# Tiles padded to 64 bytes and three norm factors moved into the exponentials' scales, in a decoder layer on one core

## The chip, the cores and the metric

One Trainium2 chip, of which one NeuronCore runs the kernel. The metric is the device time of one execution in microseconds (us); "time" of a kernel is the median of its runs. The engines are TensorE (PE in the profile, its weight loads PEld), VectorE (DVE), ScalarE (ACT), GpSimd (POOL) and SyncE (SP), which here issues nearly all DMAs.

## What is computed

The reference is one decoder layer for 256 tokens of width 1024, in float32. Cut to what matters here:

```python
hn = rmsnorm(h, mix_norm_g); proj = hn @ w_in            # q, k, v, conv, gates
h = h + concat([conformer_conv(...), nsa_mixer(q, ...)]) @ w_out
h = h + memory_attention(rmsnorm(h, g), rmsnorm(mem, g2), w_q, w_k, w_v, w_o)
h = h + peer(rmsnorm(h, peer_norm_g), w_q, sub_keys, u_emb, v_emb)
return rmsnorm(h, final_norm_g)
# in each attention: softmax((q @ k.T) * scale); in peer: top 16 of 16 x 16 candidate
# pairs for each token and head, softmax over those scores, experts u and v (16384 x 1024)
```

`rmsnorm` multiplies each token by one factor r = 1/sqrt(mean(x*x) + eps) (and each column by a gain). A query that is projected from a normed row is therefore r times the query projected from the unnormed row, and so are its scores.

## The kernel before, in words

Tokens stand in the free dimension (256 columns), features in the partitions. A product in nearly float32 precision is made of three `float32r` matmuls: every operand is split in a high part (a rounding copy on ACT) and a low part (a subtraction on DVE), and `mm3` (L151 to L154) issues high x high, low x high and high x low into one PSUM tile. `wchunk` (L147) loads 512 KB of weights into a tile `raw` and splits it in two halves (`wsplit`, L134 to L145: `hi` L141 on ACT, `lo` L142 on DVE, or on POOL where it is told so); `hi` and `lo` have six buffers each, three chunks deep. In `mm3` the weights are the stationary operand and the 256 token columns move; in the last stage (L1071) the activations `ah`, `al` are stationary and the weights move, 512 columns a matmul.

TensorE's order is the program's (a manual schedule for that engine alone); the other engines' instructions are put in order by the scheduler of the tile framework. The stages are:

- the input projection (`proj1`, plain float32 matmuls of two passes, L163) with the conformer convolution on DVE, then the sparse attention (`scores` L548, `transposes`, `weighted`), into which the key and value projections of the memory attention are filled (`filler`, L432: tiles `pmk`, `pmv`);
- `w_out` (tiles `pwo`), the queries of the memory attention (`mq_chunk`, `mq_out`, L718 to L727, tiles `pmq`), its scores `pms` (L735 to L737) and weighted sums `pmo` (through `mm3`), `w_mem_o` (tiles `pmw`);
- the 16 chunks of the expert queries (L846, tiles `ppq`), each copied out of PSUM by `pq_out` (L829) and matched with the keys by `key_scores` (L834);
- the choice of the 16 best experts on DVE (L893 to L954) while TensorE goes through the first of the 128 chunks of `u` (`u_chunk`, L987, tiles `pu`): for chunks 0 to 33 POOL makes the low parts, from chunk 34 (`JG`) on DVE does. From chunk 41 on `gates4` (L1003) comes in between for four tokens at a time: four DVE operations make one-hot tiles (L1011 to L1014), eight fp16 matmuls multiply them (L1017, L1018), and DVE and ACT put the result into `slA` and `slB` (L1022, L1023);
- 128 chunks of `v` (tiles `Y`, L1071), and the last norm.

**The norm factors.** `Rstd` sums the squares of a row; `sums` (L214) makes the column `col` with r of each token (two matmuls `ss`, a dozen DVE operations of two columns), then two diagonal matrices; `rows` (L229) multiplies them by ones (`sr`, L233), so that `row` holds r along the free dimension in all partitions. `r0` belongs to the input, `r1` to `h1`, `r2` to `h2`. Before, each query tile is multiplied by `row` as it leaves PSUM (L392, L725, L831, all on DVE). For this TensorE's program has `r1.sums()` after the first query chunk and `r1.rows()` after the third (L766, L769); `r2.sums()` and `r2.rows()` stand in the loop at L851 and L855, and `key_scores` follows two chunks behind.

**Where tiles lie.** A pool's tiles lie one behind the other in each partition, each rounded up to 32 bytes. From the left follow `cst`, `wts`, `h2p`, `tk`, then `mp`, `mwk`, and in the last stages `e1`, `tmp`. `cst` begins at a multiple of 64 bytes and holds 1088 + 1088 (`par`, 1076) + 512 + 32 (`halfpi`, 4 bytes) + 256 + 256 = 3232 bytes, 32 more than a multiple of 64. So `wts` begins 32 bytes past a multiple of 64, and since its own tiles and those of `h2p` and `tk` are all multiples of 64, so do `raw`, `hi`, `lo`, `hx`, `g1`, `gx`, `hn`, and, behind them, `mg`, `mq_h`, `mo` and (in `tmp`) `ah`, `al`. Tiles behind an odd number of further small tiles are back at a multiple of 64: `mk_h`, `mk_l` (behind `rsc_m`). The pools of the right side (`ch`, `wk`, then `tp`, `twk`) end at the top of the memory; there `nsa_h`, `cv_h`, `q_h`, `mq_l`, `mv2` and `MP` begin at multiples of 64. These addresses are the program's own, from the tile sizes.

Of the kernel before, what the change touches and what calls it, by code (L numbers as in the profile page):

```python
# [9 lines left out]
F32 = mybir.dt.float32  # L10
# [3 lines left out]
I32 = mybir.dt.int32  # L14
# [82 lines left out]
def build(tc, A, out, dbg=None):  # L97
# [5 lines left out]
    def show(name, ap):  # L103
        if dbg is not None and name in dbg:
            nc.sync.dma_start(dbg[name], ap)

    cst = outer.enter_context(tc.tile_pool(name="cst", bufs=1))
    wts = outer.enter_context(tc.tile_pool(name="wts", bufs=2))

    con1 = cst.tile([P, NCON1], F32, name="con1")  # L110
    par = cst.tile([P, NPAR], F32, name="par")

    def C(name):
        a, b = CC[name]
# [82 lines left out]
    class Rstd:  # L197
# [13 lines left out]
                self.eng.tensor_add(self.acc, self.acc, sq)  # L211
            self.k += 1

        def sums(self):  # L214
# [4 lines left out]
            m = mwk.tile([P, 2], F32, name=f"m_{self.tag}", tag="rs_m")  # L219
            V.tensor_scalar(m, ps, self.scale, EPS, op0=ALU.mult, op1=ALU.add)  # L220
            y = self.col = self.pool.tile([P, 2], F32, name=f"rsc_{self.tag}")
            t = mwk.tile([P, 2], F32, name=f"t_{self.tag}", tag="rs_t")
            sh = mwk.tile([P, 2], I32, name=f"sh_{self.tag}", tag="rs_i")
            rsqrt(y, m, t, sh)
            self.diag = mwk.tile([P, 2, P], F32, name=f"dg_{self.tag}", tag="rs_d", bufs=1)
            for hf in range(2):
                V.tensor_scalar(self.diag[:, hf], C("ident"), y[:, hf:hf + 1], None, op0=ALU.mult)
# [49 lines left out]
    V.tensor_scalar(ang, ang, PIF, -PIF, op0=ALU.min, op1=ALU.max)  # L277
    aabs = Ct = ch.tile([P, T], F32, name="Ct")
    V.scalar_tensor_tensor(aabs, ang, -1.0, ang, op0=ALU.mult, op1=ALU.max)
    halfpi = cst.tile([P, 1], F32, name="halfpi")  # L280
    V.memset(halfpi, math.pi / 2)


# [104 lines left out]
    for i in range(6):  # L388
        dst = kraw[i] if i < 2 else qraw[:, i - 2]
        ps = psum(T, f"pq{i}")  # L390
        proj1(ps, wload(A["w_in_t"][10 + i]), hx)
        V.tensor_mul(dst, ps, r0.row)  # L392
        if i >= 2:
            nc.sync.dma_start(w1[i // 2 - 1][:, 8 * (i % 2):8 * (i % 2) + 8], A["w1"][i // 2 - 1, :, 8 * (i % 2):8 * (i % 2) + 8])
        if i == 1:
            rm.sums()
        todo.append((i, dst))
        if i > 1:
            rope(*todo.pop(0))
        conv(3)  # L400
# [14 lines left out]
            rm.rows()  # L415
        conv(3)
    gate = ch.tile([P, 2, 8, 3], F32, name="gate")
    chalf = wk.tile([P, 2], F32, name="chalf", tag="bcol")
# [55 lines left out]
    for i in range(2):  # L474
        G.memset(hdn[i], 0.0)
        ph = psum(45, f"ph{i}", "at")
        phv = ph.rearrange("p (g c) -> p g c", g=3)
        for jj in range(16):
            PE.matmul(phv, w1[i][:, jj], KV[i][:, :, 2 * jj:2 * jj + 16 * (NC_CMP - 1) + 1:16],
                      start=(jj == 0), stop=(jj == 15))  # L480
            if jj % 2:
                fill(1)
        bcol = wk.tile([P, 1], F32, name=f"bcol{i}", tag="bcol")
# [27 lines left out]
    def cmp_scores(hf):  # L511
# [12 lines left out]
        S.activation(sc, sc, AF.Exp, scale=0.125)  # L524
# [23 lines left out]
    def scores(c, g, hf):  # L548
        r = slice(64 * g, 64 * g + 64)
        W = P * (hf + 1)  # L550
        sl = slice(hf * P, hf * P + P)
        ps = psum(2 * W, f"pss{c}{g}{hf}", "at").rearrange("p (b k) -> p b k", b=2)
        PE.matmul(ps, q_h[r, c, sl], k_h[r, :, 0:W], start=True, stop=False)
        PE.matmul(ps, q_h[r, c, sl], k_l[r, :, 0:W], start=False, stop=False)
        PE.matmul(ps, q_l[r, c, sl], k_h[r, :, 0:W], start=False, stop=False)
        for b in range(2):
            PE.matmul(ps[:, b, hf * P:W], identb, causb, start=False, stop=(b == 1))
        mx = wk.tile([P, 2], F32, name=f"amx{c}{g}{hf}", tag="amx", bufs=4)
        V.tensor_reduce(mx, ps, axis=AX.X, op=ALU.max)
        V.tensor_scalar(mx, mx, -0.125, None, op0=ALU.mult)  # L560
        pe = wk.tile([P, 2, T], F32, name=f"ape{c}{g}{hf}", tag="ape", bufs=3)
        sm = wk.tile([P, 2], F32, name=f"asm{c}{g}{hf}", tag="asm", bufs=4)
        for b in range(2):
            S.activation(pe[:, b, 0:W], ps[:, b], AF.Exp, scale=0.125, bias=mx[:, b:b + 1], accum_out=sm[:, b:b + 1])
# [156 lines left out]
        return ps  # L721

    def mq_out(i, ps):
        t = twk.tile([P, T], F32, name=f"mqt{i}", tag="mqt", bufs=4)
        V.tensor_mul(t, ps, r1.row)  # L725
        S.activation(mq_h[:, i], t, AF.Copy)
        V.tensor_sub(mq_l[:, i], t, mq_h[:, i].bitcast(F32))  # L727

    def m_scores(h):
        for hf in range(2):  # L730
            sl = slice(hf * P, hf * P + P)
            ps = psum(T, f"pms{h}{hf}", "at")
            for k in range(2):
# [4 lines left out]
            mx = twk.tile([P, 1], F32, name=f"mmx{h}{hf}", tag="mmx", bufs=4)  # L738
            V.tensor_reduce(mx, ps, axis=AX.X, op=ALU.max)
            V.tensor_scalar(mx, mx, -0.0625, None, op0=ALU.mult)  # L740
            sm = twk.tile([P, 1], F32, name=f"msm{h}{hf}", tag="msm", bufs=4)
            pe = mpe[h, hf] = twk.tile([P, T], F32, name=f"mpe{h}{hf}", tag="mpe", bufs=3)
            S.activation(pe, ps, AF.Exp, scale=0.0625, bias=mx, accum_out=sm)
            V.reciprocal(sm, sm)
            V.tensor_scalar(pe, pe, sm, None, op0=ALU.mult)

# [15 lines left out]
                mm3(po, [m[:, kb, i * P:(i + 1) * P] for m in mv2], *[m[:, kb] for m in MP[h]], kb == 0, kb == 1)  # L762
            split((mo_h[:, i], mo_l[:, i]), po)

    pq0 = mq_chunk(0)
    r1.sums()  # L766
    pq1 = mq_chunk(1)
    pq2 = mq_chunk(2)
    r1.rows()  # L769
    mq_out(0, pq0)  # L770
    mq_out(1, pq1)
    mq_out(2, pq2)
    for i in range(3, KC):
        mq_out(i, mq_chunk(i))
        if i == 4:
            m_scores(0)
        if i == 6:
            m_scores(1)
            m_transposes(0)
        if i == 7:  # L780
            m_weighted(0)
# [46 lines left out]

    def pq_out(i, ps):  # L829
        qt = twk.tile([P, T], F32, name=f"pqt{i}", tag="mqt", bufs=4)  # L830
        V.tensor_mul(qt, ps, r2.row)  # L831
        return qt

    def key_scores(i, qt):  # L834
# [11 lines left out]
    for i in range(16):  # L846
        ps = psum(T, f"ppq{i}")
        proj(ps, wchunk(A["peer_w_q"][i]), (gx_h, gx_l))
        todo.append((i, ps))
        if i == 0:  # L850
            r2.sums()  # L851
        if i < 2:
            continue
        if i == 2:
            r2.rows()  # L855
            todo = [(j, pq_out(j, p)) for j, p in todo]
            continue
        todo[-1] = (i, pq_out(i, ps))
        key_scores(*todo.pop(0))
        if i == 3:  # L860
            key_scores(*todo.pop(0))


# [92 lines left out]
    def choice_gates():  # L956
        for hf in range(2):
            ge = picked[hf][2]
            tc.keep_in_program_order(S.activation(ge, ge, AF.Exp))
            gs = tp.tile([P, 8], F32, name=f"gs{hf}", tag="gs")  # L960
            V.tensor_reduce(gs, ge, axis=AX.X, op=ALU.add)
            V.reciprocal(gs, gs)
# [79 lines left out]
    gfin = h2p.tile([P, D], F32, name="gfin", tag="act_l")  # L1042

    def final(nh):
        sq2 = tmp.tile([P, 2], F32, name=f"fs{nh}", tag="fs")
# [6 lines left out]
        m, h, y, t, sh = [tmp.tile([P, 1], I32 if j == 4 else F32, name=f"fm{nh}{j}", tag=f"fm{j}") for j in range(5)]  # L1052
# [118 lines left out]
```

## Time and profile before

| | |
|---|---|
| time, median of 3 runs (lowest to highest) | 1082.33 us (1081.17 to 1082.73) |
| the profiled execution: its time; span from first to last instruction | 1082.72 us; 1080.9 us |
| TensorE (PE) busy | 1061.2 us, 98%, 7346 matmul records |
| VectorE (DVE) busy | 871.8 us, 81% |
| ScalarE (ACT) busy | 580.0 us, 54% |
| GpSimd (POOL) busy | 102.3 us, 9% |
| mean granted TensorE clock | 0.996 of full speed |
| HBM read | 179.81 MB, 167 GB/s over the span |

The span is the time between the first and the last instruction; the execution's own time is 1.8 us more. Matmuls are pipelined: a record lasts longer than the distance to the next one's start, so that a rate is read from starts, not from durations. Busy shares are means over stages that differ.

### The profile page before, as it was taken

How to read it: one execution, taken by the hardware profiler on the slowest of the kernel's cores; microseconds unless marked ns; L12 is line 12 of the kernel's file. 1: busy time of each engine (PE TensorE's matmuls, PEld its weight loads, DVE VectorE, ACT ScalarE, POOL GpSimd, SP SyncE). 2: the span in 40 equal slices, each digit the busy share in tenths (PEclk: the TensorE clock that was granted, in tenths of full speed). 3: DMA queues.
4: the chain of work that ended last, by engine and by line, in shares of the span. 5: the costliest groups of instructions: out<-in, count | busy, mean ns of one | idle time of the engine just before them, and what ended most of it. 6: DMA issues, size and time to landing. Idle time of an engine off the chain costs nothing.

```text
span 1080.9 us, 20534 instructions
## 1 busy us (share of the span) xinstructions
PE 1061.2 (98%) x7346; PEld 976.3 (90%) x7346; DVE 871.8 (81%) x2226; ACT 580.0 (54%) x1334; POOL 102.3 (9%) x82
## 2 busy tenths in 40 slices
PE   8999999999999999999999999999999999999997
PEld 7889878999999999999999999998888888888885
DVE  4998888978889998889999999986666666666665
ACT  4224676566455555665555555455555555555554
POOL 0000000000039992000000000001000000000000
PEclk9999999999999999999999999999999999999999
DMA  7744333525435555444554444466555555555552
GB/s 245 247 127 151 98 99 117 196 98 174 159 116 178 178 193 167 160 162 157 162 164 163 163 150 160 156 203 201 194 190 193 194 192 192 195 194 193 195 195 78
DMA packets 51685, 182.45 MB, mean 169 GB/s; under 512 B 5760, under 2 KB 6528, under 8 KB 51456
## 3 DMA queue, kind: packets, MB, share of 16 engines
q1 hardware_dynamic: 51296, 180.62, 50.8%
q8 instruction: 58, 0.95, 0.4%
q10 hardware_dynamic: 288, 0.52, 0.1%
q14 instruction: 43, 0.35, 0.1%
HBM read 179.81 MB, written 1.05 MB: 167 GB/s over the span
## 4 chain that ended last, share of the span: by engine, by line
PE 85%; DVE 13%; ACT 1%; DMA 1%; issue 0%; SPq 0%; DVEq 0%; ACTq 0%
PE Y L1071 32%; PE pu L152 9%; PE pu L154 8%; PE pu L153 8%; PE pq L163 2%; PE pw L1017 1%; PE ppq L152 1%; PE ppq L153 1%; PE ppq L154 1%; PE pb L163 1%; PE pw L1018 1%; PE pa L163 1%; DVE ohx L948 1%; PE pmk L152 1%; DVE lo L142 1%; DVE ohx L946 1%
## 5 line engine op out<-in xcount | busy, mean ns | idle before, releaser
L141 ACT ACTIVATE hi<-raw 128x512 fp32r<-128x512 f32 x624 | 376.7, 626 | 176.7 <-PE pu L153 66.9
L142 DVE TENSOR_TENSOR lo<-raw,hi 128x512 fp32r<-128x512 f32 x556 | 369.1, 687 | 26.8 <-ACT hi L141 21.0
L152 PE MATMUL pu<-hn_h,hi 128*128 128x256 f32 x1024 | 296.3, 289 | 0.0
L154 PE MATMUL pu<-hn_h,lo 128*128 128x256 f32 x1024 | 290.7, 284 | 1.9 <-DVE lo L142 1.9
L153 PE MATMUL pu<-hn_l,hi 128*128 128x256 f32 x1024 | 290.7, 284 | 0.0
L154 PEld LDWEIGHTS pu<-hn_h,lo 128*128 128x128 f32 x1024 | 197.3, 193 | 2.1 <-DVE lo L142 2.1
L153 PEld LDWEIGHTS pu<-hn_l,hi 128*128 128x128 f32 x1024 | 197.4, 193 | 0.0
L152 PEld LDWEIGHTS pu<-hn_h,hi 128*128 128x128 f32 x1024 | 197.2, 193 | 0.0
L1071 PE MATMUL Y<-hi,al 128*128 128x512 f32 x512 | 158.3, 389 | 0.0
L1071 PE MATMUL Y<-lo,ah 128*128 128x512 f32 x512 | 158.3, 389 | 0.0
L1071 PE MATMUL Y<-hi,ah 128*128 128x512 f32 x512 | 158.2, 389 | 0.0
L1071 PEld LDWEIGHTS Y<-hi,al 128*128 128x128 f32 x512 | 96.1, 188 | 20.0
L1071 PEld LDWEIGHTS Y<-lo,ah 128*128 128x128 f32 x512 | 96.1, 188 | 19.9
L1071 PEld LDWEIGHTS Y<-hi,ah 128*128 128x128 f32 x512 | 96.1, 188 | 19.8
L167 DVE TENSOR_TENSOR al<-slB,ah 128x256 fp32r<-128x256 f32 x88 | 37.4, 425 | 86.1 <-PE Y L1071 86.1
L166 ACT ACTIVATE ah<-slB 128x256 fp32r<-128x256 f32 x88 | 36.8, 418 | 110.7 <-PE Y L1071 110.7
L142 POOL TENSOR_TENSOR lo<-raw,hi 128x512 fp32r<-128x512 f32 x68 | 94.8, 1421 | 11.8 <-ACT hi L141 9.2
L1023 ACT ACTIVATE slB<-pw 128x348 f32<-128x348 f32 (+31 forms) x64 | 32.5, 507 | 70.2 <-DVE slB L1022 57.0
L298 DVE SCALAR_TENSOR_TENSOR yc<-u,par,yc 128x256 f32<-128x256 f32 x120 | 54.8, 474 | 0.1
L167 DVE TENSOR_TENSOR al<-slA,ah 128x256 fp32r<-128x256 f32 x40 | 17.1, 428 | 37.3 <-PE Y L1071 37.3
L166 ACT ACTIVATE ah<-slA 128x256 fp32r<-128x256 f32 x40 | 16.7, 418 | 49.3 <-PE Y L1071 48.0
L152 PE MATMUL ppq<-gx_h,hi 128*128 128x256 f32 x128 | 37.4, 292 | 0.0
(372 smaller groups left out, 1745.7 us busy)
## 6 DMA issues: line engine op xcount, KB each, us to landing
raw<-u SPq DMA_DIRECT2D x128, 512.0 KB, 3.4
raw<-v SPq DMA_DIRECT2D x128, 512.0 KB, 3.3
raw<-peer_w_q SPq DMA_DIRECT2D x16, 512.0 KB, 3.3
raw<-w_in_t SPq DMA_DIRECT2D x15, 512.0 KB, 3.8
raw<-w_mem_k SPq DMA_DIRECT2D x8, 512.0 KB, 4.5
raw<-w_mem_v SPq DMA_DIRECT2D x8, 512.0 KB, 3.3
raw<-w_out SPq DMA_DIRECT2D x8, 512.0 KB, 3.4
raw<-w_mem_q SPq DMA_DIRECT2D x8, 512.0 KB, 3.5
```

The costliest lines, as they stand in the source:

```text
L141: S.activation(hi, r, AF.Copy)
L142: (engs or (V, V))[q].tensor_sub(lo, r, hi.bitcast(F32))
L152: PE.matmul(ps, w[0], xh, start=start, stop=False)
L153: PE.matmul(ps, w[0], xl, start=False, stop=False)
L154: PE.matmul(ps, w[1], xh, start=False, stop=stop)
L163: PE.matmul(ps, w[0][:, k * P:(k + 1) * P], x[:, k], start=k == 0, stop=k == KC - 1)
L166: S.activation(dst[0], src, AF.Copy)
L167: V.tensor_sub(dst[1], src, dst[0].bitcast(F32))
L298: V.scalar_tensor_tensor(yc[:, i], u[:, i, j:j + T], w, yc[:, i], op0=ALU.mult, op1=ALU.add)
L946: V.tensor_tensor(o4, o4, tif[:, side].unsqueeze(2).to_broadcast([P, 16, 16, 8]), op=ALU.mult)
L1023: S.activation(slB[:, done - J:, n0:n0 + 4].rearrange("p i n -> p n i"), pw[:, :, done:], AF.Copy, scale=1.0 / GSC)
L1071: PE.matmul(Y[nh][c], lhs[:, sl], wc[c][t], start=False, stop=i == KEYS - 1 and lhs is a[1], skip_group_check=True)
```

## The change

1. A helper `small` allocates a tile whose width is rounded up to 16 elements of four bytes, 64 bytes, and gives back the part that is used. `par`, `halfpi` and all tiles of one or two columns that stand in the diff are allocated by it, so that every tile behind them on the left side begins at a multiple of 64 bytes. (The tiles of 8 columns stay as they were; on the right side the tile `u` of 4576 bytes stays.)
2. The queries of the sparse attention, of the memory attention and of the experts are no longer multiplied by r. The exponentials get r times the old scale as a column (`r8`, `r16`, `r2c`), and the negated maximum is multiplied by the same column. `r1.rows()` is gone; `r2.rows()` comes one chunk later, for `hn` alone; `key_scores` follows one chunk behind, not two.

```diff
+    def small(pool, w, dt=F32, **kw):
+        return pool.tile([P, -(-w // 16) * 16], dt, **kw)[:, 0:w]
-    par = cst.tile([P, NPAR], F32, name="par")
+    par = small(cst, NPAR, F32, name="par")
-    halfpi = cst.tile([P, 1], F32, name="halfpi")
+    halfpi = small(cst, 1, F32, name="halfpi")
...
-        V.tensor_mul(dst, ps, r0.row)
+        if i < 2:
+            V.tensor_mul(dst, ps, r0.row)
+        else:
+            S.activation(dst, ps, AF.Copy)
...
+    r8, r8n = [small(ch, 2, name=f"r8{j}") for j in range(2)]
+    V.tensor_scalar(r8, r0.col, 0.125, None, op0=ALU.mult)
+    V.tensor_scalar(r8n, r0.col, -0.125, None, op0=ALU.mult)
...
-        V.tensor_scalar(mx, mx, -0.125, None, op0=ALU.mult)
+        V.tensor_scalar(mx, mx, r8n[:, hf:hf + 1], None, op0=ALU.mult)
...
     def mq_out(i, ps):
-        t = twk.tile([P, T], F32, name=f"mqt{i}", tag="mqt", bufs=4)
-        V.tensor_mul(t, ps, r1.row)
-        S.activation(mq_h[:, i], t, AF.Copy)
-        V.tensor_sub(mq_l[:, i], t, mq_h[:, i].bitcast(F32))
+        split((mq_h[:, i], mq_l[:, i]), ps)
...
-    pq0 = mq_chunk(0)
-    r1.sums()
-    pq1 = mq_chunk(1)
-    pq2 = mq_chunk(2)
-    r1.rows()
-    mq_out(0, pq0)
-    mq_out(1, pq1)
-    mq_out(2, pq2)
-    for i in range(3, KC):
+    r16 = [small(mp, 2, name=f"r16{j}") for j in range(2)]
+    for i in range(KC):
         mq_out(i, mq_chunk(i))
+        if i == 1:
+            r1.sums(rows=False)
+            for j in range(2):
+                V.tensor_scalar(r16[j], r1.col, (0.0625, -0.0625)[j], None, op0=ALU.mult)
...
     def pq_out(i, ps):
         qt = twk.tile([P, T], F32, name=f"pqt{i}", tag="mqt", bufs=4)
-        V.tensor_mul(qt, ps, r2.row)
+        S.activation(qt, ps, AF.Copy)
         return qt
...
-        todo.append((i, ps))
-        if i == 0:
+        todo.append((i, pq_out(i, ps)))
+        if i == 1:
             r2.sums()
-        if i < 2:
-            continue
-        if i == 2:
+            V.tensor_copy(r2c, r2.col)
+        if i == 3:
             r2.rows()
-            todo = [(j, pq_out(j, p)) for j, p in todo]
-            continue
-        todo[-1] = (i, pq_out(i, ps))
-        key_scores(*todo.pop(0))
-        if i == 3:
+        if i:
             key_scores(*todo.pop(0))
...
-            tc.keep_in_program_order(S.activation(ge, ge, AF.Exp))
+            tc.keep_in_program_order(S.activation(ge, ge, AF.Exp, scale=r2c[:, hf:hf + 1]))
```

## Rows read from the trace of the kernel before

**Rows 1.** The page, chain of work that ended last: its shares by engine.
```profile
PE 85%; DVE 13%; ACT 1%; DMA 1%; issue 0%; SPq 0%; DVEq 0%; ACTq 0%
```

**Rows 2.** Busy time by stretch (us, count), then granted clock, DMA share, GB/s.
```profile
313.00:418.00 105.00, 103.49 (x861) 102.97 (x859) 104.28 (x359) 60.84 (x118) 89.65 (x64) 1.00 0.51 166
418.00:725.00 307.00, 306.14 (x2773) 303.40 (x2774) 284.84 (x674) 169.74 (x437) 0.00 (x0) 0.99 0.50 164
725.00:1070.00 345.00, 345.00 (x1523) 285.77 (x1523) 216.11 (x378) 184.27 (x379) 2.77 (x1) 1.00 0.57 189
...
600.00:650.00 50.00, 50.00 (x459) 49.53 (x458) 49.24 (x115) 27.89 (x73) 0.00 (x0) 1.00 0.48 158
650.00:700.00 50.00, 50.00 (x463) 49.49 (x462) 50.00 (x114) 24.95 (x71) 0.00 (x0) 1.00 0.47 159
...
420.00:421.00 1.00, 1.00 (x6) 1.00 (x6) 0.98 (x3) 0.40 (x1) 0.00 (x0) 0.50 0.52 135
```

**Rows 3.** TensorE in order of time, a chunk of u: start, duration, line.
```profile
501.00 0.28 PE L152 MATMUL pu<-hn_h,hi 128*128 128x256 f32 x1
...
502.92 0.28 PE L153 MATMUL pu<-hn_l,hi 128*128 128x256 f32 x1
```

**Rows 4.** The chain that ended last, in order of time: the v stage.
```profile
725.00 344.80 PE Y L1071 x1521
```

**Rows 5.** TensorE in order of time: the weighted sums pmo.
```profile
226.52 0.28 PE L153 MATMUL pmo<-MP,mv 128*128 128x256 f32 x1
...
226.97 0.28 PE L154 MATMUL pmo<-MP,mv 128*128 128x256 f32 x1
...
238.46 0.28 PE L152 MATMUL pmo<-MP,mv 128*128 128x256 f32 x1
...
239.38 0.28 PE L154 MATMUL pmo<-MP,mv 128*128 128x256 f32 x1
```

**Rows 6.** TensorE in order of time: a chunk of w_out.
```profile
170.62 0.28 PE L153 MATMUL pwo<-nsa_l,hi 128*128 128x256 f32 x1
...
171.94 0.28 PE L152 MATMUL pwo<-nsa_h,hi 128*128 128x256 f32 x1
```

**Rows 7.** TensorE's groups by line and tile: count, busy us, mean ns.
```profile
L152 PE MATMUL pu<-hn_h,hi 128*128 128x256 f32 x1024 | 296.3, 289 | 0.0
L1071 PE MATMUL Y<-hi,al 128*128 128x512 f32 x512 | 158.3, 389 | 0.0
L152 PE MATMUL ppq<-gx_h,hi 128*128 128x256 f32 x128 | 37.4, 292 | 0.0
L152 PE MATMUL pmq<-g_h,hi 128*128 128x256 f32 x64 | 18.5, 289 | 0.0
```

**Rows 8.** TensorE in order of time, chunk 34 of u; behind it the idle time's releaser.
```profile
416.67 0.28 PE L153 MATMUL pu<-hn_l,hi 128*128 128x256 f32 x1
418.86 0.39 PE L154 MATMUL pu<-hn_h,lo 128*128 128x256 f32 x1 [1.91 <-DVE lo L142]
```

**Rows 9.** Waits of TensorE: us in total, times, longest.
```profile
PE sr_c L233 <- DVE dg_c L227: 2.3, 1, 2.3
...
PE sr_h L233 <- DVE dg_h L227: 1.4, 1, 1.4
```

**Rows 10.** DVE and TensorE in order of time: the last gates4.
```profile
711.63 0.41 DVE L1014 TENSOR_TENSOR o<-o,gTl 128x512 f16<-128x512 f16 x1
...
715.68 0.23 PE L1017 MATMUL pw<-o,o 128*128 128x128 f16 x1
```

**Rows 11.** DVE's group of the expert queries, and ACT's wait in that stretch.
```profile
L831 DVE TENSOR_TENSOR pqt<-ppq,rs_h 128x256 f32<-128x256 f32 x16 | 6.5, 416 | 3.3 <-PE ppq L154 3.3
...
ACT hi L141 <- PE ppq L153: 26.6, 27, 2.7
```

**Rows 12.** TensorE in order of time: the end of the expert queries.
```profile
312.25 1.50 PE L840 MATMUL psq<-skp,pqt 128*128 128x128 f32 x12
314.21 0.38 PE L880 MATMUL Y<-zero 128*128 128x512 bf16 x1 [0.46 <-ACT sco L843]
```

More of the change, by code (lines that the diff above doesn't have):

```diff
@@ L212, in add, with sums @@
             self.k += 1
-        def sums(self):
+        def sums(self, rows=True):
             ps = psum(2, f"ss_{self.tag}", "at")
@@ L218, in sums @@
                 PE.matmul(ps[:, hf:hf + 1], self.acc[:, hf * P:hf * P + P], ones[:, 0:1], start=True, stop=True)
-            m = mwk.tile([P, 2], F32, name=f"m_{self.tag}", tag="rs_m")
+            m = small(mwk, 2, F32, name=f"m_{self.tag}", tag="rs_m")
             V.tensor_scalar(m, ps, self.scale, EPS, op0=ALU.mult, op1=ALU.add)
-            y = self.col = self.pool.tile([P, 2], F32, name=f"rsc_{self.tag}")
-            t = mwk.tile([P, 2], F32, name=f"t_{self.tag}", tag="rs_t")
-            sh = mwk.tile([P, 2], I32, name=f"sh_{self.tag}", tag="rs_i")
+            y = self.col = small(self.pool, 2, F32, name=f"rsc_{self.tag}")
+            t = small(mwk, 2, F32, name=f"t_{self.tag}", tag="rs_t")
+            sh = small(mwk, 2, I32, name=f"sh_{self.tag}", tag="rs_i")
             rsqrt(y, m, t, sh)
+            if not rows:
+                return
             self.diag = mwk.tile([P, 2, P], F32, name=f"dg_{self.tag}", tag="rs_d", bufs=1)
@@ L417, in build @@
     gate = ch.tile([P, 2, 8, 3], F32, name="gate")
-    chalf = wk.tile([P, 2], F32, name="chalf", tag="bcol")
+    chalf = small(wk, 2, F32, name="chalf", tag="bcol")
+    r8, r8n = [small(ch, 2, name=f"r8{j}") for j in range(2)]
+    V.tensor_scalar(r8, r0.col, 0.125, None, op0=ALU.mult)
+    V.tensor_scalar(r8n, r0.col, -0.125, None, op0=ALU.mult)
     V.tensor_scalar(chalf, r0.col, 0.5, None, op0=ALU.mult)
@@ L482, in build @@
                 fill(1)
-        bcol = wk.tile([P, 1], F32, name=f"bcol{i}", tag="bcol")
+        bcol = small(wk, 1, F32, name=f"bcol{i}", tag="bcol")
         V.tensor_add(bcol, ph[:, 30:31], Pm("cmp_b1")[:, i:i + 1])
@@ L523, in cmp_scores @@
         V.tensor_tensor(sc, sc, mx.unsqueeze(2).to_broadcast([P, 8, 16]), op=ALU.subtract)
-        S.activation(sc, sc, AF.Exp, scale=0.125)
+        S.activation(sc, sc, AF.Exp, scale=r8[:, hf:hf + 1])
         sm = wk.tile([P, 8], F32, name=f"sm{hf}", tag="sm")
@@ L557, in scores @@
             PE.matmul(ps[:, b, hf * P:W], identb, causb, start=False, stop=(b == 1))
-        mx = wk.tile([P, 2], F32, name=f"amx{c}{g}{hf}", tag="amx", bufs=4)
+        mx = small(wk, 2, F32, name=f"amx{c}{g}{hf}", tag="amx", bufs=4)
         V.tensor_reduce(mx, ps, axis=AX.X, op=ALU.max)
-        V.tensor_scalar(mx, mx, -0.125, None, op0=ALU.mult)
+        V.tensor_scalar(mx, mx, r8n[:, hf:hf + 1], None, op0=ALU.mult)
         pe = wk.tile([P, 2, T], F32, name=f"ape{c}{g}{hf}", tag="ape", bufs=3)
-        sm = wk.tile([P, 2], F32, name=f"asm{c}{g}{hf}", tag="asm", bufs=4)
+        sm = small(wk, 2, F32, name=f"asm{c}{g}{hf}", tag="asm", bufs=4)
         for b in range(2):
-            S.activation(pe[:, b, 0:W], ps[:, b], AF.Exp, scale=0.125, bias=mx[:, b:b + 1], accum_out=sm[:, b:b + 1])
+            S.activation(pe[:, b, 0:W], ps[:, b], AF.Exp, scale=r8[:, hf:hf + 1], bias=mx[:, b:b + 1], accum_out=sm[:, b:b + 1])
         V.reciprocal(sm, sm)
@@ L737, in m_scores @@
                 PE.matmul(ps, mq_l[:, i, sl], mk_h[:, i], start=False, stop=(k == 1))
-            mx = twk.tile([P, 1], F32, name=f"mmx{h}{hf}", tag="mmx", bufs=4)
+            mx = small(twk, 1, F32, name=f"mmx{h}{hf}", tag="mmx", bufs=4)
             V.tensor_reduce(mx, ps, axis=AX.X, op=ALU.max)
-            V.tensor_scalar(mx, mx, -0.0625, None, op0=ALU.mult)
-            sm = twk.tile([P, 1], F32, name=f"msm{h}{hf}", tag="msm", bufs=4)
+            V.tensor_scalar(mx, mx, r16[1][:, hf:hf + 1], None, op0=ALU.mult)
+            sm = small(twk, 1, F32, name=f"msm{h}{hf}", tag="msm", bufs=4)
             pe = mpe[h, hf] = twk.tile([P, T], F32, name=f"mpe{h}{hf}", tag="mpe", bufs=3)
-            S.activation(pe, ps, AF.Exp, scale=0.0625, bias=mx, accum_out=sm)
+            S.activation(pe, ps, AF.Exp, scale=r16[0][:, hf:hf + 1], bias=mx, accum_out=sm)
             V.reciprocal(sm, sm)
@@ L821, in build @@
     show("h2", h2T)
+    r2c = small(tk, 2, name="r2c")
     skp = tp.tile([P, 16, P], F32, name="skp")
@@ L1044, in final @@
     def final(nh):
-        sq2 = tmp.tile([P, 2], F32, name=f"fs{nh}", tag="fs")
+        sq2 = small(tmp, 2, F32, name=f"fs{nh}", tag="fs")
         junk = wts.tile([P, 1024], F32, name=f"fj{nh}", tag="raw", bufs=4)
@@ L1050, in final @@
             V.tensor_mul(z[:, c * 512:c * 512 + 512], Y[nh][c], gfin[:, c * 512:c * 512 + 512])
-        m, h, y, t, sh = [tmp.tile([P, 1], I32 if j == 4 else F32, name=f"fm{nh}{j}", tag=f"fm{j}") for j in range(5)]
+        m, h, y, t, sh = [small(tmp, 1, I32 if j == 4 else F32, name=f"fm{nh}{j}", tag=f"fm{j}") for j in range(5)]
         V.tensor_scalar(m, sq2[:, 0:1], sq2[:, 1:2], D * EPS, op0=ALU.add, op1=ALU.add)
```

## The prediction, made before the changed kernel was run

> **What bounds the kernel now.** I read the page first: the chain of work that ended last is 85% TensorE and 13% DVE [rows 1], so the kernel goes at TensorE's pace except where DVE sets the end. The busy time by stretch tells where that is [rows 2]. Between 313 and 418 us DVE is busy 104.3 of 105 us with the choice of the experts; TensorE runs ahead of it through the first chunks of u, and at chunk 34, the first whose low parts DVE makes, it stands still from the end of its turn at 416.8 until 418.86, released by `lo` [rows 8]. From 418 to 725 us TensorE has no gaps and DVE is busy 284.8 of 307 us, but 49.2 and 50.0 of 50 near the end. The v stage is TensorE alone: 1521 starts in 344.8 us, 226.7 ns each [rows 4].
>
> Then I read TensorE's pace from the starts of neighbours. In a chunk of u, 16 steps take 1.92 us, 120 ns for a matmul of 256 columns [rows 3]. The clock was granted in full there, 2.4 GHz; 256 columns are 106.7 ns at that clock, so 13 ns of each are not streaming. In the v stage it is 226.7 for 512 columns, 213.3 of streaming: again 13 ns. The excess is one per matmul, not per column. One group is quicker: the weighted sums `pmo`, the same `mm3` with 256 columns, need 0.45 us for 4 steps and 0.92 us for 8, 112 to 115 ns, middle 114 [rows 5]. By the tile sizes, `pmo` is the only one of these groups whose operands both start at a multiple of 64 bytes. In `w_out` the moving operand does too (`nsa_h`, `nsa_l`) and the stationary one (`hi`, `lo`) lies 32 past: 11 steps in 1.32 us, 120 ns [rows 6]. So it is the start of the stationary operand that goes with the 6 ns.
>
> **The change, part by part.** The sum is made against the profiled execution (1082.7 us, span 1080.9), which lies 0.4 us above the median of the runs.
>
> *Starts at multiples of 64.* After the change `cst` holds 1088 + 1088 + 512 + 64 + 256 + 256 = 3264 bytes, 51 times 64. The pools behind it on the left are sums of multiples of 64, so `raw`, `hi`, `lo`, `hn`, `mg`, `ah` and `al` all lie as `pmo`'s operands do now. Each `float32r` matmul with a stationary operand now 32 past should go 6 ns quicker. For 512 columns no row shows the aligned case; the bounds are 0 and the whole 13 ns, and I take 6, because the excess is the same as with 256 columns. Counts, three lines of `mm3` to a group [rows 7]: u 3 x 1024 = 3072; v 3 x 512 = 1536; `ppq` 3 x 128 = 384; `pmq` 192, and `pmk`, `pmv`, `pmw` and `w_out` as many each.
>
> - Up to 313 us: `ppq`, `pmq`, `pmw`, `w_out` 960 x 6 = 5.8 us. `pmk` and `pmv` 384 x 6 = 2.3 us, but they fill the sparse attention, where TensorE ends in a wait for DVE's norm (2.3 us, [rows 9]); what is saved just ahead of it only lengthens it. I keep 1.7. Together 7.5.
> - 313 to 418 us: the 34 chunks hold 816 matmuls, 4.9 us. DVE's choice starts when the last expert query is there and is as long as before, and chunk 34 still waits for it. So the 4.9 us go into that wait, which grows from 2.0 to about 7: I count 0.
> - 418 to 725 us: 94 chunks, 2256 x 6 = 13.5 us. Here DVE is late next. Per chunk there are 24 `float32r` and 64 x 8 / 85 = 6 fp16 matmuls, so of the 459 records in 50 us 367 get quicker, 2.2 us. DVE has 0.8 us idle at 600 to 650 and none at 650 to 700 [rows 2]; it falls behind by 1.4 + 2.2 + 0.7 (up to 716 us) = 4.3 us more than today. Its reserve at the last `gates4` is the distance from the end of `ol` at 712.04 to the matmul at 715.68, 3.6 us [rows 10]. So TensorE waits some 0.7 us, and a little for late low parts: I take 1.2, bounds 0 and 4.3. Left: 12.3.
> - v stage: 1536 x 6 = 9.2 us. Nothing else is near its limit there: of 345 us DVE is busy 216 and ACT 184 [rows 2].
>
> The plain float32 matmuls (`proj1`, transposes) and the fp16 ones I count at nothing; `small` itself adds no instruction.
>
> *Norm factors.* `r1.rows()` goes: TensorE's wait of 1.4 us for the diagonal [rows 9], and four records of 128 columns; twelve such take 1.5 us [rows 12], so 0.4. Saved 1.8; at least 0, if low parts are late next. What replaces it (two tiny DVE operations for `r16`) is needed only at the first `m_scores`, three chunks later. DVE loses 16 multiplications of 416 ns [rows 11] and 8 + 4 of the same size; DVE has idle time there and no wait of TensorE's is released by them, so I count 0. ACT gains 4 + 16 copies out of PSUM; their cover is ACT's own idle time, 26.6 us of waiting for TensorE in the stretch of the expert queries [rows 11]; without that cover 16 x 0.42 = 7 us would be late, on ACT. The scales as columns in place of constants cost nothing: the same instructions read them. `key_scores` one chunk behind: at the end only the last one is left and it has to wait for its own copy, where before another one stood in between. Twelve records lie there in 1.5 us [rows 12]; four fewer, so 0.4 us lost.
>
> *The clock.* Behind the wait at chunk 34 the granted clock was 0.50, that is 1.2 GHz in its last row [rows 2]; six matmuls start in that us in place of eight. TensorE had been idle for 2 us ahead of it. After the change it idles for 7. I count the same drop again, 0, and allow 3 us more of it, 1 us.
>
> Sum: 7.5 + 0 + 12.3 + 9.2 + 1.8 - 0.4 = 30.4 us. 1082.7 - 30.4 = 1052.3, less 0.4 for the median: **1052 us**.
>
> **The rivals.**
>
> *A, the start does not matter.* `pmo` is quicker for another reason: it is short, and its operands lie in the right-hand pools. Then only the norm factors count: 1082.3 - 1.8 + 0.4 = 1081 us, no change. For it speaks that 44 such steps are a small sample; against it that `w_out` and `pmo` differ in nothing else that I find in the code. The Trainium skill, "SBUF — State Buffer", section "Specifications (TRN2)", gives lines of 16 bytes as what an access pays for crossing; by that a start 32 past a multiple of 64 is already on a line, and A holds. The rows on `pmo` speak against that.
>
> *B, the whole excess goes.* 11 of the 13 ns: 1344 x 11 = 14.8 us early on, v 16.9, and between 418 and 725 us the 2256 x 11 = 24.8 would put TensorE at 282 us, under DVE's 284.8, so DVE bounds it and about 18 are left. With the 1.4 us of the norm factors: 1082.3 - 51 = 1031 us. Against it: `pmo` is aligned and still has 7 ns of excess. The Trainium skill, "TensorE: Matmul & The Clock Gate", section "Wait — 56ns, not 53.3ns?", has a fixed cost of about 2.5 ns for each matmul at full clock, which would be B; no row of the float32r groups here comes near it.
>
> *C, DVE becomes the bound of the u stage.* TensorE would meet DVE at every `gates4`, not only at the last, since idle time that DVE has early (22 of 307 us) does not all lie where it can be used. Half of the 13.5 us go, at worst all: 1058 to 1064 us. For it the two full windows of DVE; against it the reserve of 3.6 us even at the last one.
>
> *D, slower: the copies wait in ACT's queue.* ACT works in order, and while the expert queries run it stands before a `hi` until TensorE frees the buffer, 27 times, up to 2.7 us [rows 11]. If `pq_out` stands behind such a `hi`, TensorE's `key_scores`, now one chunk behind, waits for it, and so does the next `hi`: a loop. At 2.7 us for each of 16 chunks that is 43 us, 1095 us in all. It decides from 30.4 / 16 = 1.9 us a chunk on. Against it: the scheduler has a whole chunk (2.9 us) for one copy.
>
> That an odd tile is left over and the change does not do what it says, is excluded by the sum of the sizes on the left; on the right `PT` and `con2` come to lie 32 past, but they feed only plain float32 matmuls.
>
> **How the numbers follow.** Forecast 0.78, C 0.10, A 0.07, B 0.03, D 0.02. Own range of the forecast: with 7 ns a matmul 1376 + 2256 + 1536 = 5168 matmuls (32 of `pms` with them) give 36 us, with the 1.8 together 38, so 1044; with 5 ns, nothing in the v stage, 3 us of DVE and 1 of the clock, 18.2 + 1.8 - 0.4 - 3 - 1 = 16, so 1066. C lies inside; A, B and D are left out with 0.12. Range 1044 to 1066. A measurement of this kernel can tell about 0.2%, 2.2 us, from no change. Faster: the forecast, C and B, 0.91; same: A, 0.07; slower: D, 0.02.
>
> **What would show it.** Right: steps of 114 ns in u and of about 221 in v, with the v stage some 9 us shorter; TensorE's wait at chunk 34 near 7 us and DVE still busy throughout the choice; no `sr_h` in the memory attention; DVE full from about 600 us on and a wait of TensorE's of a us or so near the end of u. Wrong: steps still 120 (A) or 109 (B); TensorE waiting for `o` or `lo` all through the second half of u (C); `psq` waiting for `pqt` in every chunk (D); or steps of 227 in v beside 114 in u, which would mean that the excess of the wide matmuls is another.

## The result, and the profile after

The changed kernel takes 1088.28 us (median of 4 runs, 1087.86 to 1088.92), the kernel before 1081.94 on the same chip: ratio 1.0052, interval 1.0039 to 1.0064. It is **slower by 0.5%**, where I had forecast a gain of 2.8%. Of the signs that I had named under "wrong" the first came, steps still 120 in u; steps that get longer I had not thought of.

The chain of waits in order of time shows the loss in one row, the v stage (start, us, engine, tile, line, count):

```profile
719.92 354.92 PE Y L1075 x1521
```

Beside [rows 4] that is 10.1 us more for as many starts: 233.3 ns each, not 226.7. In TensorE's rows in order of time two matmuls together take 0.47 us where they took 0.45:

```profile
800.50 0.63 PE L1075 MATMUL Y<-hi,al 128*128 128x512 f32 x2
800.97 0.63 PE L1075 MATMUL Y<-hi,ah 128*128 128x512 f32 x2
```

By stretch (us; busy time of PE, PEld, DVE, ACT, POOL; then clock, DMA share, GB/s), with the windows of [rows 2], TensorE has no gap from 418 to 725 us and a clock granted in full. (The stages begin some 5 us earlier in the changed kernel, so this window ends with the first 5 us of v, and its count of 2773 records, the same as before, says nothing of the pace. That u did not get quicker the table below shows.) And v is longer though its clock is granted in full as well (1.00 up to its last start at 1078 us; the 0.99 takes in the 8 us behind it):

```profile
418.00:725.00 307.00, 307.00 (x2773) 303.25 (x2773) 282.80 (x667) 171.32 (x440) 0.00 (x0) 1.00 0.52 166
725.00:1086.00 361.00, 353.33 (x1515) 284.35 (x1513) 220.39 (x399) 185.69 (x383) 2.78 (x1) 0.99 0.57 180
```

TensorE's waits (us in total, times, longest), beside [rows 9]: the diagonal `sr_h` of the memory attention is gone, as forecast; the wait at chunk 34 is 2.2 us, not 7; `psq` waits for the copy `pqt` once.

```profile
PE pu L158 <- DVE lo L146: 2.2, 1, 2.2
...
PE sr_c L239 <- DVE dg_c L233: 1.9, 1, 1.9
...
PE Y L884 <- ACT sco L852: 0.9, 1, 0.9
...
PE psq L849 <- ACT pqt L840: 0.4, 1, 0.4
```

From the starts of the stages' first matmuls (us between them; the two last columns are experiments 3 and 4):

| from, to | before | after | norms alone | starts alone |
|---|---|---|---|---|
| `pmk` to `w_out` (sparse attention) | 91.35 | 88.62 | 89.36 | 90.53 |
| `w_out` to `ppq` (memory attention) | 89.23 | 86.87 | 87.23 | 88.36 |
| `ppq` to the first `Y<-zero`, 4.3 us ahead of chunk 0 of u | 54.56 | 55.82 | 55.82 | 54.64 |
| to chunk 34 | 102.34 | 102.33 | 102.33 | 102.33 |
| chunk 34 to v | 308.29 | 308.63 | 308.31 | 308.63 |
| v, first to last start | 347.96 | 358.17 | 347.96 | 358.17 |

From `pmk` up to u the change gains 3.8 us, in u it loses 0.3, and v costs 10.2. (What lies ahead of `pmk` took 76.8 to 81.6 us in the profiled executions here, 79.1 before and 77.5 after, and is left out. With these 1.6 us the sum is the 5.1 us by which the span grew, 1080.9 to 1086.0.)

### The profile page after: what moved, and what is told of

Its sections match the earlier page's. It is cut to its first block, busy times and chain, and to the rows that moved or that the text cites. A ratio compares the mean times of both kernels' runs of the same rounds, so it can differ in the third digit from the quotient of the medians.

```text
span 1086.0 us, 20527 instructions
## 1 busy us (share of the span) xinstructions
PE 1067.7 (98%) x7341; PEld 972.3 (90%) x7342; DVE 864.8 (80%) x2201; ACT 588.0 (54%) x1353; POOL 101.2 (9%) x82
## 4 chain that ended last, share of the span: by engine, by line
PE 87%; DVE 12%; DMA 1%; ACT 0%; issue 0%; SPq 0%; DVEq 0%
PE Y L1075 33%; PE pu L156 9%; PE pu L158 8%; PE pu L157 8%; PE pq L167 2%; PE pw L1021 1%; PE ppq L157 1%; PE ppq L156 1%; PE ppq L158 1%; PE pw L1022 1%; PE pb L167 1%; PE pa L167 1%; DVE ohx L952 1%; PE pmk L156 1%; PE pmw L157 1%; DVE ohx L950 1%
## 5 line engine op out<-in xcount | busy, mean ns | idle before, releaser
L1075 PE MATMUL Y<-lo,ah 128*128 128x512 f32 x512 | 161.5, 396 | 0.0
L1075 PE MATMUL Y<-hi,al 128*128 128x512 f32 x512 | 161.5, 395 | 0.0
L1075 PE MATMUL Y<-hi,ah 128*128 128x512 f32 x512 | 161.4, 396 | 0.0
```

The costliest lines, as they stand in the source:

```text
L1075: PE.matmul(Y[nh][c], lhs[:, sl], wc[c][t], start=False, stop=i == KEYS - 1 and lhs is a[1], skip_group_check=True)
```

## The experiments

**Theory.** After the result I looked for what the starts have in common in the quick and the slow groups, and found the *distance*: how far the stationary operand starts behind the moving one in the partition, modulo 256 bytes. By the sizes of the tiles it is 0 before in all groups of the sum but `w_out`, 160, and in `pmo` 64. The change leaves it at 0 in u, `ppq` and `pmq`, and makes it 64 in v. Rivals: the starts themselves; when the transfers land; what stands ahead in the queue.

**1. The disputed cost by itself.** Series of 64 `float32r` matmuls at each distance, with both operands moved by 32 bytes too. Nothing of the reference is computed.

```python
m0 = phase + 256 * (k % 5)          # phase 0, or 8 elements
s0 = 8 * d + 128 * (k % 7)          # d: 32 bytes a step
PE.matmul(y[:, 0:width], sta[:, s0:s0 + P], mov[:, m0:m0 + width], ...)
```

> This kernel computes nothing of the layer: it writes zeros and runs series of 64 float32r matmuls whose stationary operand begins 0, 32, ... 480 bytes further than the moving one, modulo 512, with 256 and with 512 columns, the moving one at a multiple of 64 and once more 32 past it. Theory (the distance decides): the step from one start to the next changes with the distance, by steps of 6.7 ns: about 120 ns and 227 ns at distance 0, 233 ns at 64 for 512 columns, and near 113 ns at 320 for 256 columns; moving both tiles by 32 changes nothing. Rival (the start itself decides): all distances that are multiples of 64 give one step, those 32 past another, and with both tiles moved by 32 it is again another.

One tile's rows (durations of a record, then the first and the last start of 64; `o` and `x`: both at a multiple of 64, and both moved; last letter: a 0, c 64 bytes of distance):

```profile
L47 PE MATMUL woa<-mov,sta x64: 389/389/397, 202.1 to 216.4; 128*128 128x512 f32 x64
L47 PE MATMUL woc<-mov,sta x64: 393/396/398, 231.5 to 246.2; 128*128 128x512 f32 x64
L47 PE MATMUL wxa<-mov,sta x64: 387/389/397, 439.6 to 453.9; 128*128 128x512 f32 x64
L47 PE MATMUL wxc<-mov,sta x64: 390/396/398, 454.2 to 468.9; 128*128 128x512 f32 x64
```

14.3 us for 63 steps is 227 ns, 14.7 is 233, and moving both by 32 bytes changes neither. Over all distances, ns a step:

| distance mod 256 | 0 | 32 | 64 | 96 | 128 | 160 | 192 | 224 |
|---|---|---|---|---|---|---|---|---|
| 256 columns | 119.9 | 118.3 | 117.8 | 117.4 | 118.5 | 119.9 | 117.8 | 116.8 |
| 512 columns | 226.9 | 233.3 | 233.4 | 234.1 | 232.4 | 233.3 | 229.1 | 233.3 |

From 256 bytes on it repeats. So 0 is the best distance for wide matmuls and one of the two worst for narrow ones; `w_out`'s 160 is the other.

**2. The distance of v back to 0**, all starts still at multiples of 64:

```diff
     tmp = outer.enter_context(tc.tile_pool(name="tmp", ...))
+    tmp.tile([P, 112], F32, name="gap", bufs=1)
```

> The changed kernel with 448 bytes more ahead of the tiles of the v stage, so that all tiles still begin at multiples of 64 but ah and al lie at the same place modulo 512 as hi and lo again. Theory (the distance decides): steps of 227 ns in the v stage, the stage 10 us shorter, 1078 us in all. Rival (a start at a multiple of 64 slows wide matmuls): still 233 ns and 1088 us. Rival (the transfers of v land later, 4.3 in place of 3.3 us, and that slows the stage): still 233 ns.

1076.41 us, ratio 0.994 (0.9924 to 0.9957). The chain's row for v:

```profile
720.62 344.80 PE Y L1076 x1521
```

344.80 us is to the hundredth what it was before. The whole loss in v goes with that distance.

**3, 4. The two parts apart.** First the norm factors without the padding, then the padding without the norm factors:

```diff
-        return pool.tile([P, -(-w // 16) * 16], dt, **kw)[:, 0:w]
+        return pool.tile([P, w], dt, **kw)
```

> The norm factors in the exponentials' scales as in the changed kernel, but no tile padded (r2c put with the tiles of the right side, so that the left side lies as in the kernel before). Theory: v steps of 227 and u steps of 120 as before; 2.0 us gained at r1.rows, about 1.5 us lost at the end of the expert queries, so 1081 to 1082 us. Rival (the slowdown comes from the norm factors): 1086 to 1088 us.

> The kernel before with the tiles of the left side padded to 64 bytes as in the changed kernel, the norms as before. Theory: v steps of 233 ns, 10 us lost there, some 3 us gained in pmk, pmv, w_out and pmw, so 1088 to 1090 us. Rival (the slowdown comes from the norm factors): 1079 to 1082 us.

Norms alone: 1078.83 us, ratio 0.9964 (0.995 to 0.9978). Starts alone: 1090.15, ratio 1.0078 (1.0056 to 1.01), v again 354.91 us in the chain. The change is a gain and a larger loss, and the columns of the table above show where each lies. "Norms alone" is not quite that: two of its new small tiles (`r8`, `r8n`) move the tiles of the right side by 64 bytes, `w_out` comes to distance 224 and to 116.7 ns a step, and 0.6 us of its gain up to `ppq` is from there.

**5. Can `mm3` and v do better?** Series in `mm3`'s order and in v's, at many pairs of distances for the high and the low parts.

> Computes nothing of the layer: it writes zeros and runs two series in the order of the real stages. First the three matmuls of mm3 (wh x xh, wh x xl, wl x xh, 256 columns, 48 to a series) with the weights 0, 32, ... 224 bytes further than the activations modulo 256, and the low parts 0, 64, 128 or 192 bytes further than the high ones on either side; then the order of the v stage (one stationary half for two moving tiles of 512 columns), with the stationary side, its low part and the second moving tile 0, 64, 128 or 192 bytes further. Theory (each step is set by the distance between the moving operand and the next stationary one): the mean of a series is the mean of its three distances in the curve measured before, so 117 to 120 ns in mm3, and 226.7 ns as the least in the v order. Rival (what came before counts too): some series reach 114 ns, as pmo does in the kernel, and some of the v order may go below 226 ns.

In `mm3`'s order distance 0 takes 119.9 ns, 64 takes 113.8, the best pair 113.3 and the worst 121.0. In v's order the best pair takes 227.2. So the order counts too: 64 gives 117.8 in a plain series. And it gives `pmo` its 114: distance 64.

**6. Is it modulo 256?** As experiment 2 with a gap of 192 bytes (`[P, 48]`), distance 256 in v.

> The changed kernel with 192 bytes ahead of the tiles of the v stage in place of 448: ah and al then lie 256 bytes, not 0 or 512, from the place of hi and lo. Theory (the distance decides, and the curve repeats every 256 bytes): v steps of 227 ns, 1076 to 1078 us as with 448. Rival (the period is 512): 233 ns, 1086 to 1088 us.

1078.52 us in one run, v 344.80 us in the chain as in experiment 2. With this the rival of the transfers falls: a load of v lands after 4.3 us (median) in the changed kernel and in experiments 2 and 6 alike, and after 3.3 us before and in experiment 4, where v takes 354.91.

**7, 8, 9. Distance 64 in u and 0 in v.** The kernel after with a gap in `h2p`; the same with another in `mp`; and the kernel *before* with two gaps and nothing else, where `hi` still starts 32 past a multiple of 64:

```diff
     h2p = outer.enter_context(tc.tile_pool(name="h2p", bufs=1))
+    h2p.tile([P, 48], F32, name="gap", bufs=1)
```

> The kernel after, with a gap of 192 bytes at the front of h2p: hi and lo now start 64 past hn modulo 256 (before and after: 0), ah and al at the same place modulo 256 as hi; every start is still a multiple of 64. Theory (the distance between the stationary and the moving operand modulo 256 sets the excess, 64 in the order of mm3 gives 114 ns for 256 columns, 0 gives 227 for 512): steps of u and of the expert queries 114 ns, of v 227; u after chunk 34 shorter by 94 x 24 x 6 = 13.5 us less what DVE cannot follow (0 to 4), the expert queries 2.4 us shorter, TensorE's wait at chunk 34 some 5 us longer; 1058 to 1064 us. Rival (what came before decides, not the distance): u 120 ns, 1076. Rival (DVE bounds the second half of u): steps of 114 in a chunk but waits of TensorE on o or lo between them, 1066 to 1074.

> As the run before it, with another gap of 192 bytes in mp, so that the pools of the sparse and the memory attention behind it move as well, and the matmuls that have hi and lo over mg, mo or their like lie 64 apart, not 0. Theory: pmk, pmw and pmq go from 117 to 120 to about 114 ns where their distance becomes 64; 384 to 576 of them by 3 to 6 ns are 1 to 3 us before 313 us, and u and v as in the run before; 1056 to 1063 us, 0 to 3 us below it. Rival (distance counts only in mm3's u order): no difference from the run before it.

> The kernel before, with nothing of the change: starts 32 past multiples of 64, norms where they were, and only two gaps, 192 bytes at the front of h2p and 64 in tmp, which set the same distances as in the first run of this call (u 64, v 0 modulo 256). Theory: steps of u 114 and of v 227 ns though hi starts at 288 modulo 512, which is no multiple of 64; some 3.5 to 4.5 us slower than the first run of this call (the norm factors' share, 1082.7 less 1078.8), 1062 to 1068 us. Rival (a start at a multiple of 64 is needed for 114 ns): 120 ns in u, 1082. Rival (the norm factors gain nothing once u is quick): as the first run.

1075.42 us, ratio 0.9928 (0.9905 to 0.9951); **1073.27**, ratio 0.9912 (0.9888 to 0.9936), the best of all; and 1085.19, ratio 0.9976 (0.9937 to 1.0014), no clear change, with two groups of times, 1073 to 1077 and 1084 to 1089. The first two are faster than both kernels but miss what I expected (1058 to 1064 and 1056 to 1063). TensorE's rows of experiment 7 in order of time tell why, first in the 5th chunk of u, then in the 60th or so (15 steps each):

```profile
330.19 0.28 PE L156 MATMUL pu<-hn_h,hi 128*128 128x256 f32 x1
...
331.89 0.28 PE L156 MATMUL pu<-hn_h,hi 128*128 128x256 f32 x1
...
500.29 0.28 PE L156 MATMUL pu<-hn_h,hi 128*128 128x256 f32 x1
...
502.06 0.28 PE L156 MATMUL pu<-hn_h,hi 128*128 128x256 f32 x1
```

1.70 us is 113.3 ns a step, 1.77 us 118. The first 34 chunks go at 113.3 throughout; from chunk 35 on (in experiment 8 from chunk 38) nearly all go at 117.8. In the third kernel, too, the first 34 go at 113.3, with `hi` at 288 modulo 512: a start at a multiple of 64 is not needed. What the quicker chunks gain there (102.3 us less 96.9) goes mostly into the wait of chunk 34, as the prediction said it would:

```profile
PE pu L158 <- DVE lo L146: 6.3, 1, 6.3
```

The two groups of the third kernel may have another cause. Its profiled execution (1087.3 us, of the slower group) has these rows of DVE, in the choice of the experts, and of POOL:

```profile
384.62 19.69 DVE L908 CAST tif<-tix 128x128 f16<-128x128 uint32 x1
...
401.60 2.57 POOL L142 TENSOR_TENSOR lo<-raw,hi 128x512 fp32r<-128x512 f32 x2
```

The choice has four such casts. The shortest, the median and the longest (ns) are:

```profile
L908 DVE CAST tif<-tix x4: 260/1098/19687, 321.5 to 405.7; 128x128 f16<-128x128 uint32 x4
```

0.26 us is the one at 405.7, with POOL at rest; the long one lasts until POOL's last two low parts end (2.57 us from 401.60, so at 404.17). The choice ends later by that, and waits of TensorE's of 7.9 and 8.4 us follow. No execution of the quicker group was profiled, so that the long cast makes the two groups is not shown.

That a cast waits for POOL the traces do show. In the ten profiled executions with these casts on DVE, 39 of the 40 ran beside POOL's low parts, and each ended 0.13 to 0.15 us behind the end of one: 34 behind the first low part that ended after the cast's start, three behind the second (2.2 us), one behind the sixth (7.2 us, in experiment 13) and this one behind the 16th. The Trainium skill, "SBUF — State Buffer", section "SBUF: two separate sides", has a DVE instruction that needs the pair of ports shared with GpSimd and a GpSimd instruction shut each other out by an exclusive lock, held for a whole instruction. The 34 fit that, with low parts of 1.4 us on POOL; that a cast is passed over as many as 15 times does not follow from it, and the reason stays open.

**10. What decides between 113 and 118.** Chunks as in u, at distance 0 and 64, with breaks of short fp16 matmuls as the gates make them; and 512 columns.

```python
brk = [()] + [(P,) * k for k in (1, 2, 3, 4, 6, 8)] + [(P,) * 8 + (e,) for e in (16, 32, ...)]
```

> The kernel computes nothing of the reference: chunks of 24 matmuls in the order of mm3 (256 columns), between them a break of 0 to 8 fp16 matmuls of 128 columns, or of 8 and one narrower one, ten chunks for each, at distance 0 and at distance 64; then chunks of 24 matmuls of 512 columns without a break and with one of 8. Theory (at distance 64 there are two paces, 113.3 and 117.8 ns, and a break decides which of them holds until the next break; at distance 0 there is one): at distance 64 whole chunks at 113.3 beside whole chunks at 117.8, all at 113.3 without a break; at distance 0 120 ns whatever the break; 512 columns 226.7 at distance 0 and 233.3 at 64 whatever the break. Rival (the pace of 117.8 in the second half of u comes from DVE, ACT or the transfers): 113.3 in every chunk at distance 64 whatever the break.

TensorE in order of time, without a break (27 steps), then a chunk between breaks of six (18 steps):

```profile
505.74 0.28 PE L54 MATMUL uca<-X,W 128*128 128x256 f32 x1
...
508.80 0.28 PE L54 MATMUL uca<-X,W 128*128 128x256 f32 x1
...
642.19 0.51 PE L58 MATMUL z<-H 128*128 128x128 f16 x6
...
642.83 0.28 PE L56 MATMUL ucf<-X,W 128*128 128x256 f32 x1
...
644.95 0.28 PE L56 MATMUL ucf<-X,W 128*128 128x256 f32 x1
```

3.06 / 27 is 113.3, 2.12 / 18 is 117.8. At distance 64 breaks of 4, 6 and 8 leave the next chunk at 118, breaks of 1, 2, 3 and 9 at 113, each chunk as a whole, with no other engine at work. At distance 0 every chunk takes 120. With 512 columns, tried without a break and with one of eight, the steps are 233.3 at distance 64 either way; at distance 0 they are 226.7, but some 231 in the first ten behind a break.

**11, 12. The cast moved to ACT**, in the kernels of experiments 9 and 8:

```diff
-            V.tensor_copy(tif[:, side], tix[:, side::2].rearrange(...))
+            S.activation(tif[:, side], tix[:, side::2].rearrange(...), AF.Copy)
```

> The kernel of the run e7_before_gaps with one edit: the four casts tif of the choice are made by ACT in place of DVE. In that run's trace one of them took 19.7 us on DVE, until POOL's row of low parts ended, and the times fell into two groups, 1073 to 1077 and 1084 to 1089. Theory (DVE's cast waits while POOL goes from one low part to the next without a gap): no time of the slower group is left, all runs 1072 to 1078, chunk 34 released some 105 us after the first Y. Rival (the two groups have another cause): both groups again, median about 1080.

> The kernel of the run e6_h2p_mp_192 with the same edit. Theory: the one time of 1083 among that run's ten does not come back, and DVE's choice is shorter by the 4.5 us that its four casts took, which chunk 34's wait (6.3 us) gives on: 1068 to 1073 us. Rival (the casts on ACT come later than DVE needs them, or a longer reserve does not count): 1073 as before.

Both worse: 1090.67 and 1087.95 us, ratios 1.0073 (1.0048 to 1.0098) and 1.0045 (1.0025 to 1.0064). The edit put a new wait in place of the old one, by ACT's waits:

```profile
ACT tif L908 <- DVE tix L904: 26.8, 2, 26.4
```

ACT works in order; the cast stood in its queue for 26.4 us until DVE had its input, behind it the `hi` of u, and TensorE waited 20.2 us for one. That is the mechanism of my rival D, at another place. What the long cast costs these two runs therefore don't tell.

**13. A break of nine in the kernel** of experiment 8:

```diff
-            PE.matmul(pw[:, j], o1[:, q, :, r], ol[:, q, :, r], start=False, stop=True)
+            for c0, c1 in ((0, P - 16), (P - 16, P)) if j == 3 else ((0, P),):
+                PE.matmul(pw[:, j, c0:c1], o1[:, q, :, r], ol[:, q, c0:c1, r], start=False, stop=c1 == P)
```

> The kernel of the run e6_h2p_mp_192 with one edit: the eighth matmul of the gates' break between chunks of u is cut into one of 112 columns and one of 16, so that the break has nine. Theory (at distance 64 a break of eight leaves the chunk after it at 117.8 ns and one of nine at 113.3): steps of 113.3 in the chunks after chunk 40 where that run has 117.8; TensorE's share of the stretch from 440 to 700 us is 4.5 x 24 = 0.11 us a chunk shorter, some 9 us in all, of which DVE, already busy 50.0 of 50 us from 650 to 700, lets 2 to 7 through; 1066 to 1071 us, with waits of TensorE for o or lo that were not there. Rival (the pace after a break in this kernel has another cause than the count of its matmuls): 117.8 as before, 1073 to 1075.

1075.69 us, ratio 0.9942 (0.9909 to 0.9975): nothing gained, steps of 118 as before. But in this execution the first 34 chunks went at 118 from the start, and of the later ones chunk 37, chunk 39 (each behind a break of two transposes) and chunk 40 at 113. In the kernels with u at distance 64 the pace changes behind breaks or behind a wait of TensorE's (in experiment 7 from 113.3 to 117.8 at chunk 34, where no other matmul comes between), and not to the same side in every execution.

**14. The break's operands.** Breaks of 8 and 9 as in experiment 10, and with operands read with every second element, as the gates do, at eight pairs of starts.

> The kernel computes nothing of the reference: chunks of 24 matmuls of 256 columns in the order of mm3 at distance 64, with breaks of 4 to 10 fp16 matmuls on contiguous operands, then of 8 and 9 on operands read with every second element, as the gates of the kernel read them, at eight pairs of starts. Theory (the operands of the break decide, not its count alone): the contiguous breaks as in micro_break (8 leaves 118 ns, 9 leaves 113), and among the breaks with every second element some of nine that leave 118, as in e10_nine. Rival (count alone decides, and e10_nine had another reason): 8 leaves 118 and 9 leaves 113 in every pair.

Contiguous: 5 and 9 leave 113, 4, 6, 8 and 10 leave 118, 7 goes to and fro. With every second element 8 leaves 113 in four pairs of starts, 118 in two, goes to and fro in one, and in one all but a chunk are at 113; 9 is as mixed (113 in four, with one chunk at 118 among them, 118 in three, one to and fro). So the operands of the break count beside its number, and a break of nine is no cure.

## Why the prediction was wrong, and where it was right

**The step that failed** is the last of the reading of the pace: "So it is the start of the stationary operand that goes with the 6 ns", with rival A's "`w_out` and `pmo` differ in nothing else that I find in the code". The rows were read rightly: 120, 114, 226.7, one excess per matmul. But `w_out` and `pmo` differ in the distance of the two operands as well (160 and 64), and I had compared each operand's start with a fixed grid, never one with the other. Experiment 1 gives 119.9 ns at 160, which is `w_out`'s 120, and experiment 5 gives 113.8 at 64, which is `pmo`'s 114. In the changed kernel all these operands start at multiples of 64, and u, `ppq` and `pmq`, still at distance 0, still take 120.

The trace of the kernel before held rows that speak against that step. By the sizes of the tiles all `float32r` operands of the sparse attention's scores (`pss`) begin at multiples of 64 there, at distance 0. From their second to their third matmul they take 117 to 120 ns with 256 columns and 229 to 240 with 512, in eight cases each (on 64 partitions, unlike the other groups):

```profile
110.90 0.39 PE L554 MATMUL pss<-k_l,q_h 64*128 64x512 f32 x1
111.13 0.39 PE L555 MATMUL pss<-k_h,q_l 64*128 64x512 f32 x1
```

So "no row shows the aligned case" for 512 columns was an oversight too.

Term by term:

- **u, 12.3 us forecast:** 0.3 us lost. Distance 0 before and after. At 64 it is to be had in part: experiments 7 and 8.
- **v, 9.2 us forecast:** 10.2 lost, 1536 by 6.65 ns. The bounds that I gave, a gain of 0 to 13 ns a matmul, excluded a loss, and I had no row for that: none shows 512 columns at another distance. A bound on the side of a loss was missing, and the range failed with it.
- **Up to 313 us, 7.5 us forecast:** experiment 4 gains 1.6 us from `pmk` to the first `Y<-zero`, and by distance too: `pmk` and `pmw` came to 192 (119.4 and 119.9 ns a step to 117.8), `pmv` to 64 (119.4 to 115.6), `w_out` to 192 and 224 there, 64 and 96 in the change (120 to 117.5); `pmq` and `ppq` stayed. (The 224 and the 96 are `cv_l`, which the change leaves 32 past a multiple of 64; my list of such tiles on the right side lacks it.)
- **The norm factors, 1.8 less 0.4 forecast:** in experiment 3 the stretch from the first `pmq` to the first `pms`, in which `r1.rows()` stood, is 2.1 us shorter, right. (From `w_out` to `ppq` it gains 2.0 in all: 0.6 more by `w_out`'s distance, 0.7 lost again behind `pms` in a handful of waits.) In the sparse attention another 2.0, which I had costed at nothing: TensorE's wait at `pmu` behind DVE's work on the sums `asm` (1.1 us) is gone and that for the norm (2.3 us, [rows 9]) is 1.8; in experiment 4, without the norm factors, both are there (1.2 and 2.4). "No wait of TensorE's is released by" the lost multiplications was the error, as I read it: they stood on DVE ahead of what does release one. The stage of the expert queries got 1.3 us longer where I had 0.4; 0.7 of that lies at its end, where TensorE waits 0.4 us for `pqt` and 0.9 in place of 0.5 for `sco`, and the rest I did not trace. In experiment 3's profile these come to 2.7 us of 4.3; the rest lies ahead of `pmk`.
- **The wait at chunk 34:** untested by the change, right in experiment 7: what the first chunks gain is lost again in the wait, 6.3 us long. The clock behind it, costed at 0 to 1 us more: 17 slow steps there cost 1.7 us and 18 in the kernel before 1.6, so some 0.1 more.
- **DVE late next (4.3 against 3.6 us of reserve, and rival C):** never reached, since u did not come to 114 in its second half. TensorE's waits in experiments 7 and 13 hold none for `o`.
- **Rival A** (the start does not matter, 1081) was right on the start and wrong on the time, for v moved. The Trainium skill, "SBUF — State Buffer", section "Specifications (TRN2)", has lines of 16 bytes, by which a start 32 past a multiple of 64 is no worse than one at it. So far the runs agree, for moving both operands by 32 bytes changed neither 227 nor 233 ns in experiment 1; I had set `pmo`'s rows against it. D did not come: `psq` waits 0.4 us once.

What stays open: why the excess depends on the distance, and whether it is the distance to a matmul's own weights or to the next one's; why a break or a wait leaves one pace or the other at distance 64; why a cast is passed over by as many as 15 low parts, and whether that makes the two groups of times; and, since experiment 9's two groups hide it, what the norm factors are worth beside the gaps.

## What to carry to other kernels

Before a rate is put down to where one operand lies, list *all* that differs between the quick and the slow group, the operands' places relative to each other among them, and measure the cost by itself: one small kernel would have settled it. A change of layout moves every tile behind it, so each of its effects wants a bound on both sides of nothing. Take the norm factors without the padding (ratio 0.9964), or with gaps that put the narrow matmuls' operands 64 apart and the wide ones' at 0 (0.9912), and look at the steps again after any edit that adds a small tile.

## What the runs showed that I had not expected

- The step of a `float32r` matmul with its own weights goes with the distance between its operands modulo 256 bytes: 113.3 to 121.0 ns for 256 columns, 226.7 to 234.6 for 512, in series with no other engine at work. The wide and the narrow want different distances.
- At distance 64 there are two paces, 113.3 and 117.8 ns. A break or a wait sets which, and it then holds for 34 chunks, 816 matmuls, if nothing comes between.
- Waits of 1.9 to 2.3 us at chunk 34 were followed by 18 long steps, most of 213 ns in place of 120 (granted clock 0.50, [rows 2]), in four kernels, and by a single one of 222 ns in those of experiments 2 and 6, where the clock stayed at 1.00: 1.6 us or 0.1.
- A cast on DVE (0.26 us with POOL at rest, mostly 0.8 to 1.4 beside it) took 7.2 and 19.7 us beside a busy POOL in one profiled execution each, and always ended just behind one of POOL's instructions.
